# Attention's steps interleaved by hand with its output projection, and layer two's plain products dealt out anew

## Chip, cores and metric

One core of one Trainium2 chip runs the whole program in one launch. The metric is the device time in microseconds (us) of that launch. Engines: TensorE (PE) multiplies matrices, VectorE (DVE), ScalarE (ACT) and GpSimd (POOL) work on elements, SyncE (SP) issues most DMAs. Each engine runs its own instructions strictly in their order and waits at an instruction until what it needs is there.

## What is computed

An inference step of a two-layer encoder, for a prompt of 2048 tokens and, with its own states and caches, a sample of 32 tokens; width 1024. Layer one is a gated delta rule with a short convolution; it isn't touched here. Layer two is attention over a window of chunks of 64 tokens (the own chunk and the two before it), 16 query heads on 4 shared key/value heads of 64 numbers, with a learned sink in each softmax and a gate:

```python
def sink_softmax(s, sinks):
    sk = sinks.astype(jnp.float32)[..., None, None]
    m = jnp.maximum(s.max(-1, keepdims=True), sk)
    p = jnp.exp(s - m)
    return p / (p.sum(-1, keepdims=True) + jnp.exp(sk - m))
...
def swa_layer(x, k, v, pos, cached, w_in, sinks, w_out, ln_g, ln_b):
    b, l, _ = x.shape
    proj = x @ w_in
    q = rope_partial(proj[..., :B_QW].reshape(b, l, B_Q_HEADS, B_HD), pos) * (B_HD ** -0.5)
    q = q.reshape(b, l, B_KV_HEADS, B_GROUP, B_HD)
    z = proj[..., B_QW:]
    sk = sinks.reshape(B_KV_HEADS, B_GROUP)
    o = cached_attention(q, k, v, sk) if cached else banded_attention(q, k, v, sk)
    out = (o * jax.nn.silu(z)) @ w_out
    return layer_norm(DN_ALPHA * x + out, ln_g, ln_b)
```

## The kernel before

**Stages.** Layer one's projections run to about 600 us, the delta rule to about 1190, layer one's output projection, together with layer two's products, to about 1763, attention with layer two's output projection to the end. The program is written piece by piece and a scheduler orders each engine's instructions, except inside a `manual_schedule` of an engine, where the order of the code holds.

**Layer two's products** (class `P2`). The results are ten units: four of the gate z (`z`, 0 to 3), four of the queries (`q`), one of the keys (`k`), one of the values (`v`), each for five blocks of 416 tokens. Block 0 is done *plainly*: a unit is 4 steps of 12 matmuls 128x416 (`product`, L1279 to L1281; each product of two split numbers takes three matmuls: high with high, low with high, high with low). Blocks 1 and 2, and blocks 3 and 4, are done as *pairs* with seven products in place of eight; their operands xs_h, xs_l are first prepared by VectorE and ScalarE (`load_pair`). Weights come through a ring of 12 tiles (`load`, ScalarE's DMA queue). `sequence` lists the units, and the generator `late` hands them out step by step: three plain z units, all of the first pair, z3, k and q0 plainly, the second pair, and at the end q1, q2, q3 and v plainly. The call `both(a, b)` runs a's steps between those of the preparation b. The plain steps at the end are spread over attention's first four chunks.

**Attention** (class `Attention`). Chunks are done in the order 10 to 31, then 0 to 9. `load_kv` brings keys (`kT`) and values (`vd`); `start` brings, for two chunks at a time, queries (`qs`) and gates (`zs`). `chunk(n)` goes through p = 0, 1 (two key/value heads each):

- scores S (L1612): four matmuls in 64-row halves, 128 query rows against 192 keys;
- `softmax`: VectorE's maximum nm (L1487, L1488), ScalarE's four exponentials P (L1495) with their sums, VectorE's es and sm (L1496 to L1499: the sink's share, the sum and its reciprocal);
- GpSimd multiplies P by the reciprocal (L1620, two of 128x384);
- TensorE transposes P (L1627, two groups of three), ScalarE copies one group (L1629), VectorE the other (L1631);
- values ot (L1633): three matmuls of 128 columns against `vd`, in which each chunk's values stand twice, on a diagonal, beside zeros;
- VectorE multiplies by the gate into graw (L1636).

Two chunks make a tile of 128 tokens, put on `pend`. `flush(keep)` then calls `finish` for the oldest tile: ScalarE rounds g_hi (L1508), GpSimd takes g_lo (L1509); for each of two halves of 512 columns TensorE does 8 x 3 matmuls 128x512 into po (L1520 to L1522), VectorE adds the residual (L1523) and takes statistics (L1524); then the normalization (helper lines L466 and L468 for its power, nb L1530, ScalarE's r L1531) and GpSimd's two multiplications with the tables (L1532, L1533) and the store of y. po has one bank of PSUM (pool `u_pp`, one buffer), so a half can't begin before L1523 of the half before has read it. The last tile's end is done by VectorE (L1537, L1539). The sample comes behind chunk 9. The scheduler places all of this, TensorE's order too. The output weights (16 pieces of 128x1024) and the tables load through SyncE's queue when the products' pools are closed (`open_right`).

Of the kernel before, what the change touches and what calls it, by code (L numbers as in the profile page):

```python
# [1133 lines left out]
class P2:  # L1134
# [10 lines left out]
    def __init__(self, tc, right, mid, I, O, T, G):  # L1145
# [108 lines left out]
    def load(self, most=2):  # L1254

        for _ in range(most):
            if self.loads and len(self.held) < self.RING:
                what, slot = self.loads.pop(0)
                w = self.wp.tile([128, 2, 4, 128], F32R, tag="w", name="w")
                src = self.T["w2"][UNITS.index(what[:2]), SLOTS.index(slot)]  # L1260
                self.nc.scalar.dma_start(w[:].rearrange("p s k c -> p s (k c)").bitcast(F32), src)
                self.held.append((what, slot, w))
# [20 lines left out]
    def units(self, units):  # L1283

        self.loads = [(u, s) for u in units for s in self.slots(u)]
        self.held = []
# [139 lines left out]
class Attention:  # L1426


    def __init__(self, tc, left, I, O, T, G):
# [9 lines left out]
        self.turn = 0  # L1439
        self.kT = one.tile([128, 2, NP], F32, tag="kT", name="kT")  # L1440

        self.vd = one.tile([128, 32, 2, 128], F32, tag="vd", name="vd")
        self.nsk = one.tile([128, 8], F32, tag="nsk", name="nsk")
# [7 lines left out]
        self.pend = []  # L1451
        self.data = {}

    def open_right(self, right):
        tc, I = self.tc, self.I
# [5 lines left out]
        rest = load_out_weights(self.nc, self.oone, self.T["wo"][1], self.nc.sync)  # L1461
        self.w = next(rest)
        drain(rest)

    def tables(self):
        self.tabs = ln_tables(self.nc, self.oone, self.I["b_ln_g"], self.I["b_ln_b"])

    def load_kv(self, a, z):
        nc, T = self.nc, self.T
        nc.sync.dma_start(self.kT[:, :, a * 64:z * 64], T["bk"][:, :, a * 64:z * 64].rearrange("a p t -> p a t"))  # L1470
        src = T["bv"][0:NP, :].rearrange("(c k) (p d) -> k c p d", k=64, p=2)
# [6 lines left out]
    def scores_tile(self):  # L1478
        self.turn += 1
        return self.ps_s[self.turn % len(self.ps_s)].tile([128, 2, 2, 256], F32, tag="S", name="S")  # L1480

    def softmax(self, S, P, nskc):
# [3 lines left out]
        nm = thr.tile([128, 4], F32, tag="nm", name="nm")  # L1486
        V.tensor_reduce(out=nm[:, :nsub], in_=S, axis=AX.X, op=ALU.max, negate=True)  # L1487
        V.tensor_tensor(out=nm[:, :nsub], in0=nm[:, :nsub], in1=nskc, op=ALU.min)  # L1488
        sm = thr.tile([128, 4], F32, tag="sm", name="sm")
        es_ = thr.tile([128, 4], F32, tag="es", name="es")  # L1490
        for u in range(nsub):
            src = S[:, u, :]
            if len(P[u].shape) == 3:
                src = src.rearrange("r (j k) -> r j k", k=64)
            nc.scalar.activation(P[u], src, AF.Exp, bias=nm[:, u:u + 1], scale=1.0, accum_out=sm[:, u:u + 1])  # L1495
# [6 lines left out]
    def finish(self, t0, n, graw, late=False, tail=False):  # L1502
        nc, V, pool = self.nc, self.nc.vector, self.otwo
# [5 lines left out]
        nc.gpsimd.tensor_tensor(out=glo[:, :, :n], in0=graw[:, :, :n], in1=ghi[:, :, :n], op=ALU.subtract)  # L1509
        st = pool.tile([128, 2, 6], F32, tag="st", name="st")  # L1510
        w, tabs = self.w, self.tabs
        both = self.scores_tile() if late else None
        for c in range(2):
            cs = slice(c * 512, c * 512 + 512)
            if late:
# [3 lines left out]
            for k in range(KC):  # L1519
                nc.tensor.matmul(ps[:n], ghi[:, k, :n], w[0][k][:, cs], start=(k == 0), stop=False)  # L1520
                nc.tensor.matmul(ps[:n], ghi[:, k, :n], w[1][k][:, cs], start=False, stop=False)  # L1521
                nc.tensor.matmul(ps[:n], glo[:, k, :n], w[0][k][:, cs], start=False, stop=(k == KC - 1))  # L1522
            V.scalar_tensor_tensor(out=r[:n, cs], in0=r[:n, cs], scalar=ALPHA, in1=ps[:n], op0=ALU.mult, op1=ALU.add)  # L1523
            V.bn_stats(out=st[:n, c, :], in_=r[:n, cs])  # L1524
        mv = pool.tile([128, 2], F32, tag="mv", name="mv")
        V.bn_aggr(out=mv[:n], in_=st[:n])
        rs = rsqrt_power(nc, self.G, pool, mv[:n, 1:2], n, 1, "ln", LN_EPS)
        if not tail:
# [4 lines left out]
            nc.gpsimd.tensor_tensor(out=r[:n], in0=r[:n], in1=tabs[1][:n], op=ALU.add)  # L1533
        else:
            for c in range(2):
                cs = slice(c * 512, c * 512 + 512)
                V.scalar_tensor_tensor(out=r[:n, cs], in0=r[:n, cs], scalar=mv[:n, 0:1], in1=tabs[0][:n, cs],  # L1537
                                       op0=ALU.subtract, op1=ALU.mult)
                V.scalar_tensor_tensor(out=r[:n, cs], in0=r[:n, cs], scalar=rs[:n, 0:1], in1=tabs[1][:n, cs],  # L1539
                                       op0=ALU.mult, op1=ALU.add)  # L1540
        nc.sync.dma_start(self.O["y"][t0:t0 + n, :], r[:n])

    def sample(self):
        nc, V, I, T = self.nc, self.nc.vector, self.I, self.T
        one, two, thr, ident = self.one, self.two, self.thr, self.G["ident"]
        ks = one.tile([128, 2, 160], F32, tag="ks", name="ks")
        nc.sync.dma_start(ks[:, :, 0:128], I["cache_kT"].rearrange("a p t -> p a t"))
        nc.sync.dma_start(ks[:, :, 128:160], T["bk"][:, :, NP:NT].rearrange("a p t -> p a t"))
        vc = one.tile([128, 256], F32, tag="vc", name="vc")
        nc.sync.dma_start(vc[:], I["cache_v"])  # L1550
        vn = one.tile([32, 256], F32, tag="vn", name="vn")
        nc.sync.dma_start(vn[:], T["bv"][NP:NT, :])
        qs = two.tile([128, 8, NS], F32, tag="qs", name="qs")
        zs = two.tile([128, 8, 128], F32, tag="zs", name="zs")
        nc.sync.dma_start(qs[:], T["bq"][:, :, NP:NT].rearrange("h p t -> p h t"))
        nc.sync.dma_start(zs[:, :, :NS], T["bz"][:, :, NP:NT].rearrange("h p t -> p h t"))
        graw = thr.tile([128, 8, 128], F32, tag="graw", name="graw", bufs=4)
        for p in range(2):
            ot = self.ps_o.tile([128, 2, 2, 128], F32, tag="ot", name="ot")
            S = self.scores_tile()  # L1560
            for half in range(2):
                hs = slice(half * 64, half * 64 + 64)
                nc.tensor.matmul(S[:, half, 0, :160], qs[hs, p * 4:p * 4 + 4, :], ks[hs, p, :], start=True, stop=True)
            P = thr.tile([128, 2, 384], F32, tag="P", name="P")
            sm = self.softmax(S[:, :, 0, :160], [P[:, 0, :160], P[:, 1, :160]], self.sks[:, p * 2:p * 2 + 2])
            nc.gpsimd.tensor_tensor(out=P[:, :, :160], in0=P[:, :, :160],
                                    in1=sm[:, 0:2].unsqueeze(2).to_broadcast([128, 2, 160]), op=ALU.mult)
            for half in range(2):
                g = p * 2 + half
                hs = slice(half * 64, half * 64 + 64)  # L1570
                gs = slice(g * 64, g * 64 + 64)
                tr = self.ps_t.tile([128, 3, 128], F32, tag="tr", name="tr")
                pt = thr.tile([128, 6, 128], F32, tag="pt", name="pt")
                nc.tensor.transpose(tr[:, 0, :], P[:, half, 0:128], ident[:, :])
                nc.tensor.transpose(tr[:32, 1, :], P[:, half, 128:160], ident[:, :])
                nc.scalar.copy(pt[:, 0, :], tr[:, 0, :])
                V.tensor_copy(pt[:32, 1, :], tr[:32, 1, :])
                oo = ot[hs, 0, 0, :]
                nc.tensor.matmul(oo, vc[:, gs], pt[:, 0, :], start=True, stop=False)
                nc.tensor.matmul(oo, vn[:, gs], pt[:32, 1, :], start=False, stop=True)  # L1580
            of = ot[:, 0, 0, :].rearrange("p (t k) -> p t k", t=4)
            V.tensor_tensor(out=graw[:, p * 4:p * 4 + 4, :NS], in0=of, in1=zs[:, p * 4:p * 4 + 4, :NS], op=ALU.mult)
        self.pend.append((NP, NS, graw))

    def start(self, n):

        nc, T = self.nc, self.T
        if n % 2 == 0:
            qs = self.two.tile([128, 2, 8, 64], F32, tag="qs", name="qs")
            zs = self.two.tile([128, 8, 128], F32, tag="zs", name="zs")  # L1590
            for i in range(2):
                tk = (n + i) * 64
                nc.sync.dma_start(qs[:, i], T["bq"][:, :, tk:tk + 64].rearrange("h p t -> p h t"))
            nc.sync.dma_start(zs[:], T["bz"][:, :, n * 64:n * 64 + 128].rearrange("h p t -> p h t"))
            graw = self.thr.tile([128, 8, 128], F32, tag="graw", name="graw", bufs=4)
            self.data = qs, zs, graw

    def chunk(self, n):
# [38 lines left out]
        if n % 2 == 1:  # L1637
            self.pend.append(((n - 1) * 64, 128, graw))
# [285 lines left out]
```

## Time and profile before

| | us |
|---|---|
| three runs | 2213.85, 2208.47, 2205.18 |
| median | 2208.47 |
| the profiled execution's own time | 2207.43 |
| its span, first to last instruction | 2205.6 |
| TensorE busy in the span | 2101.2 (95%) |
| VectorE, ScalarE, GpSimd busy | 1486.4, 912.1, 713.6 |
| mean granted TensorE clock | 0.987 |

Columns of the profile's lines: in the table by stretch a row has the stretch, its length, then busy time and instruction count of PE, of PE's weight loads, DVE, ACT and POOL, the TensorE clock that was granted (1 is full speed), the DMA engines' share and GB/s. A row of the grouped view has line, engine, operation, output and inputs, shape, count, then busy time, mean ns of one, and the engine's idle time just before it with what ended it. Rows of the timeline and of the chain have start, length and what ran; SPq is SyncE's queue, issuing DMAs. A matmul's listed length contains its passage through the array; the distance between starts is what it costs in a row of them.

### The profile page before, as it was taken

How to read it: one execution, taken by the hardware profiler on the slowest of the kernel's cores; microseconds unless marked ns; L12 is line 12 of the kernel's file. 1: busy time of each engine (PE TensorE's matmuls, PEld its weight loads, DVE VectorE, ACT ScalarE, POOL GpSimd, SP SyncE). 2: the span in 40 equal slices, each digit the busy share in tenths (PEclk: the TensorE clock that was granted, in tenths of full speed). 3: DMA queues.
4: the chain of work that ended last, by engine and by line, in shares of the span. 5: the costliest groups of instructions: out<-in, count | busy, mean ns of one | idle time of the engine just before them, and what ended most of it. 6: DMA issues, size and time to landing. Idle time of an engine off the chain costs nothing.

```text
span 2205.6 us, 37189 instructions
## 1 busy us (share of the span) xinstructions
PE 2101.2 (95%) x13370; PEld 1911.0 (87%) x13370; DVE 1486.4 (67%) x2771; ACT 912.1 (41%) x2405; POOL 713.6 (32%) x1176
## 2 busy tenths in 40 slices
PE   8999999999989999998888999899899988999997
PEld 6999999999979899887776888899899976888775
DVE  5889877776557589888865665555835566556663
ACT  5545545544412477677741111311311135444441
POOL 1212211161111288788841210000000025565663
PEclk9999999999999999999999999999999999999999
DMA  7756656567765635436737765888788895333321
GB/s 282 225 185 195 222 168 196 178 192 239 245 213 158 209 130 172 159 124 208 225 108 262 231 205 167 298 280 283 266 278 279 276 301 137 106 87 96 89 79 43
DMA packets 348377, 430.00 MB, mean 195 GB/s; under 512 B 78352, under 2 KB 276080, under 8 KB 348176
## 3 DMA queue, kind: packets, MB, share of 16 engines
q1 hardware_dynamic: 311280, 310.22, 44.3%
q10 hardware_dynamic: 36912, 117.40, 16.0%
q8 instruction: 106, 1.74, 0.3%
q14 instruction: 79, 0.65, 0.1%
HBM read 269.45 MB, written 158.44 MB: 194 GB/s over the span
## 4 chain that ended last, share of the span: by engine, by line
PE 69%; DVE 12%; POOL 5%; DMA 5%; ACT 4%; issue 3%; SPq 1%; ACTq 0%; DVEq 0%; POOLq 0%
PE ps L77 7%; PE ps L79 7%; PE ps L78 7%; PE ps L1279 5%; PE ps L1280 5%; PE ps L1281 5%; PE ot L1633 3%; PE po L1520 3%; PE po L1521 3%; PE S L1612 3%; PE po L1522 3%; PE po L1052 2%; PE po L1054 2%; PE po L1053 2%; PE tr L1627 2%
## 5 line engine op out<-in xcount | busy, mean ns | idle before, releaser
L77 PE MATMUL ps<-act_hi,w_hi 128*128 128x416 f32 x1280 | 457.2, 357 | 9.5 <-ACT w_hi L53 3.6
L79 PE MATMUL ps<-act_hi,w_lo 128*128 128x416 f32 x1280 | 449.5, 352 | 4.2 <-POOL w_lo L54 3.5
L78 PE MATMUL ps<-act_lo,w_hi 128*128 128x416 f32 x1280 | 450.0, 352 | 0.0
L77 PEld LDWEIGHTS ps<-act_hi,w_hi 128*128 128x128 f32 x1280 | 241.2, 188 | 13.7 <-ACT w_hi L53 4.2
L79 PEld LDWEIGHTS ps<-act_hi,w_lo 128*128 128x128 f32 x1280 | 241.2, 188 | 8.9 <-POOL w_lo L54 4.7
L78 PEld LDWEIGHTS ps<-act_lo,w_hi 128*128 128x128 f32 x1280 | 241.7, 189 | 2.7
L1279 PE MATMUL ps<-xs_h,w 128*128 128x416 f32 x560 | 200.0, 357 | 11.6 <-DVE ra L1336 7.6
L1280 PE MATMUL ps<-xs_l,w 128*128 128x416 f32 x560 | 200.3, 358 | 2.9 <-DVE xs_l L1182 2.9
L1281 PE MATMUL ps<-xs_h,w 128*128 128x416 f32 x560 | 198.9, 355 | 0.0
L54 POOL TENSOR_TENSOR w_lo<-w_raw,w_hi 128x1024 fp32r<-128x1024 f32 x32 | 81.0, 2530 | 357.6 <-ACT w_hi L53 343.6
L295 DVE SCALAR_TENSOR_TENSOR y<-R,convw,y 128x2083 f32<-128x2083 f32 (+2 forms) x78 | 175.3, 2247 | 24.4 <-ACT y L293 24.2
L585 POOL TENSOR_TENSOR tm<-L,Tt 128x60 f32<-128x60 f32 (+19 forms) x375 | 136.3, 363 | 87.2 <-PE sp L760 50.0
L588 POOL TENSOR_TENSOR Tt<-Tt,tm 128x60 f32<-128x60 f32 (+19 forms) x375 | 143.8, 383 | 28.3
L1620 POOL TENSOR_TENSOR P<-P,sm 128x384 f32<-128x384 f32 (+2 forms) x128 | 100.9, 810 | 120.4 <-DVE sm L1499 56.9
L1474 POOL MEMSET vd<- 64x768 f32 (+2 forms) x10 | 7.8, 779 | 398.2 <-DVE ra L1336 397.9
L1495 ACT ACTIVATE P<-S,nm 128x192 f32<-128x192 f32 (+2 forms) x260 | 104.8, 420 | 61.6 <-DVE nm L1488 49.0
L1279 PEld LDWEIGHTS ps<-xs_h,w 128*128 128x128 f32 x560 | 106.8, 191 | 14.6 <-DVE ra L1336 8.3
L1336 DVE SCALAR_TENSOR_TENSOR ra<-ps,u 128x416 f32<-128x416 f32 x60 | 35.4, 590 | 123.3 <-PE ps L1281 121.9
L1052 PE MATMUL po<-wo,g_hi 128*128 128x512 f32 (+1 forms) x272 | 111.0, 408 | 6.9 <-DVE r L1057 6.0
L1280 PEld LDWEIGHTS ps<-xs_l,w 128*128 128x128 f32 x560 | 106.5, 190 | 5.6 <-DVE xs_l L1182 4.2
L1281 PEld LDWEIGHTS ps<-xs_h,w 128*128 128x128 f32 x560 | 107.2, 191 | 1.3
L1054 PE MATMUL po<-wo,g_lo 128*128 128x512 f32 (+1 forms) x272 | 107.4, 395 | 0.0
(298 smaller groups left out, 4755.5 us busy)
## 6 DMA issues: line engine op xcount, KB each, us to landing
w<-s_w ACTq DMA_DIRECT2D x180, 512.0 KB, 4.7
s_w<-pre_hl SPq DMA_DIRECT2D x160, 256.0 KB, 2.5
w_raw<-in_w_in SPq DMA_DIRECT2D x32, 512.0 KB, 6.5
s_wo<-pre_hl SPq DMA_DIRECT2D x64, 256.0 KB, 4.0
gb<-s_gcum SPq DMA_DIRECT2D x34, 256.0 KB, 5.1
k<-s_k SPq DMA_DIRECT2D x34, 256.0 KB, 3.7
s_z<-z SPq DMA_DIRECT2D x40, 208.0 KB, 2.0
s_q<-y SPq DMA_DIRECT2D x8, 1024.0 KB, 5.2
```

The source lines that it names most:

```text
L77: nc.tensor.matmul(ps, hi[:, k, :], xh[:, k, :], start=(k == 0), stop=False)
L78: nc.tensor.matmul(ps, hi[:, k, :], xl[:, k, :], start=False, stop=False)
L79: nc.tensor.matmul(ps, lo[:, k, :], xh[:, k, :], start=False, stop=(k == KC - 1))
L295: self.nc.vector.scalar_tensor_tensor(out=y[:, a:z], in0=R[:, a + j:z + j], scalar=self.convw[:, i, j:j + 1], in1=y[:, a:z], op0=ALU.mult, ...
L585: P.tensor_tensor(out=tm[:n, i0 - k:, :w], in0=L[:n, i0:, j:j + 1].to_broadcast(sh), in1=Tt[:n, j:j + 1, :w].to_broadcast(sh), op=ALU.mult)
L588: P.tensor_tensor(out=Tt[:n, i0:, :w], in0=Tt[:n, i0:, :w], in1=tm[:n, i0 - k:, :w], op=ALU.subtract)
L1052: nc.tensor.matmul(ps[:n], ghi[:, k, :n], w[0][k][:, cs], start=(k == 0), stop=False)
L1054: nc.tensor.matmul(ps[:n], glo[:, k, :n], w[0][k][:, cs], start=False, stop=(k == KC - 1))
L1279: nc.tensor.matmul(ps, w[:, 0, k], xh[:], start=first and k == 0, stop=False, skip_group_check=True)
L1280: nc.tensor.matmul(ps, w[:, 0, k], xl[:], start=False, stop=False, skip_group_check=True)
L1281: nc.tensor.matmul(ps, w[:, 1, k], xh[:], start=False, stop=last and k == 3, skip_group_check=True)
L1495: nc.scalar.activation(P[u], src, AF.Exp, bias=nm[:, u:u + 1], scale=1.0, accum_out=sm[:, u:u + 1])
```

## The change

It does three things.

1. *Plain units.* All four z units come ahead of the first pair, ten of their steps beside its preparation (six before); v, k and q0 come ahead of the second pair; q1, q2 and q3 remain for attention.
2. *Output weights.* The ring of weight tiles lives to the end; behind the last unit's weights it takes 12 of the 16 pieces of output weights, so that `open_right` loads 4 pieces and the tables.
3. *Attention.* `chunk` is taken apart into `scores`, `turn` (transposes and copies) and `values`, and TensorE's order is written out by hand for the whole stage. Chunks 10, 11 and 12 run beside the remaining plain steps (`alone`). From chunk 13 on, `beside(n)` gives TensorE the scores of chunk n for both p, six po matmuls, `turn(n-1, 0)`, six po, `turn(n-1, 1)`, six po, `values(n-1)`, six po. The other engines' order is still the scheduler's. Values take two matmuls per pair of chunks (`vp`, 128 keys, no zeros, a new load of 2 MB in all) and two for the single chunk (`vd`), each of 64 columns, the two in different halves of the columns. GpSimd's multiplies become one of 128x4x128 and one of 128x2x2x64 for each p. The sample stands between chunk 31 and chunk 0. g_hi and g_lo are made half a tile ahead (`ready`). The last tile's y is stored in halves through two queues.

The diff, cut (`start`, `softmax` and the sample's branches keep what they computed):

```diff
@@ P2
+        self.wp = new_pool(tc, ring, "p2_w", self.RING, side="right")
-        self.wp = new_pool(tc, right, "p2_w", self.RING, side="right")
...
+                if what is None:
+                    flat = w[:].rearrange("p s k c -> p (s k c)")
+                    self.nc.scalar.dma_start(flat.bitcast(F32), self.T["wo"][1][slot // 2, :, slot % 2])
+                    self.out.append(flat)
...
-        self.loads = [(u, s) for u in units for s in self.slots(u)]
+        self.loads = [(u, s) for u in units for s in self.slots(u)] + [(None, i) for i in range(self.RING)]
@@ Attention
+        both = T["bv"][a * 64:z * 64, :].rearrange("(c k) d -> k c d", k=128)
+        nc.sync.dma_start(self.vp[:, a // 2:z // 2, :], both)
...
+                if pair is not None:
+                    part = flat[:, :, at:at + 128]
+                    nc.gpsimd.tensor_tensor(out=part, in0=part, in1=sm[:].unsqueeze(2).to_broadcast([128, 4, 128]),
+                                            op=ALU.mult)
...
+    def values(self, n):
...
+                if pair is not None:
+                    for h in range(2):
+                        hs = slice(h * 64, h * 64 + 64)
+                        nc.tensor.matmul(ot[hs, p], self.vp[:, pair, p * 128 + h * 64:p * 128 + h * 64 + 64],
+                                         pt[:, 2 * h:2 * h + 2, :], start=True, stop=one is None)
+                if one is not None:
+                    for h in range(2):
+                        hs = slice(h * 64, h * 64 + 64)
+                        nc.tensor.matmul(ot[hs, p], self.vd[:, one, p, hs], pt[:, 4:6, :],
+                                         start=pair is None, stop=True)
...
+    def alone(self, n):
+
+        self.scores(n, (0,))
+        for f in self.left_over[:1]:
+            f()
+        yield
+        for f in self.left_over[1:]:
+            f()
+        yield
+        self.scores(n, (1,))
+        self.turn(n, 0)
+        yield
+        self.left_over = [lambda: self.turn(n, 1), lambda: self.values(n)]
+        yield
+
+    def beside(self, n):
+
+        self.scores(n)
+        next(self.out)
+        for f in self.left_over:
+            f()
+            next(self.out)
+        self.left_over = [lambda: self.turn(n, 0), lambda: self.turn(n, 1), lambda: self.values(n)]
...
+            for j in self.finish(*got, last):
+                if j >= 4 and ahead is None and self.pend:
+                    ahead = self.ready()
+                yield
...
+                if k % 2 == 1 and k < KC - 1:
+                    yield 4 * c + k // 2
             V.scalar_tensor_tensor(out=r[:n, cs], in0=r[:n, cs], scalar=ALPHA, in1=ps[:n], op0=ALU.mult, op1=ALU.add)
             V.bn_stats(out=st[:n, c, :], in_=r[:n, cs])
+            if c == 0:
+                yield 3
@@ the stage
-    sequence = [("z", j, 0) for j in range(3)] + [p + (1,) for p in pairs]
-    sequence += [("z", 3, 0), ("k", 0, 0), ("q", 0, 0)] + [p + (2,) for p in pairs]
-    sequence += [("q", j, 0) for j in range(1, 4)] + [("v", 0, 0)]
+    sequence = [("z", j, 0) for j in range(4)] + [p + (1,) for p in pairs]
+    sequence += [("v", 0, 0), ("k", 0, 0), ("q", 0, 0)] + [p + (2,) for p in pairs]
+    sequence += [("q", j, 0) for j in range(1, 4)]
...
-        both(itertools.islice(late, 6), p2.load_pair(1))
+        both(itertools.islice(late, 10), p2.load_pair(1))
...
-    order = list(range(10, 32)) + list(range(10))
...
+    order = list(range(10, 32)) + ["s"] + list(range(10))
+    with tc.manual_schedule(engines={ET.PE}):
+        drain(itertools.islice(late, 2))
+        for i in range(3):
+            for _ in att.alone(order.pop(0)):
+                drain(itertools.islice(late, 1))
+            att.load_kv(*((14, 18), (18, 24), (24, 32))[i])
+        drain(late)
+        p2.rest()
+        right.close()
+        att.open_right(right, p2.out)
+        att.load_kv(0, 8)
+        for n in order:
+            att.beside(n)
+        att.rest()
```

More of the change, by code (lines that the diff above doesn't have):

```diff
@@ L1504, in finish, with rest, ready @@
+    def rest(self):
+        for f in self.left_over:
+            f()
+            next(self.out)
+        self.late = True
+        drain(self.out)
+    def ready(self):
+        nc, pool = self.nc, self.otwo
+        t0, n, graw = self.pend.pop(0)
         r = pool.tile([128, D], F32, tag="r", name="r")
@@ L1509, in finish, with outs @@
         nc.gpsimd.tensor_tensor(out=glo[:, :, :n], in0=graw[:, :, :n], in1=ghi[:, :, :n], op=ALU.subtract)
+        return t0, n, r, ghi, glo
+    def outs(self):
+        while not self.pend:
+            yield
+        got = self.ready()
+        while got is not None:
+            ahead = None
+            last = self.late and not self.pend
+            for j in self.finish(*got, last):
+                if j >= 4 and ahead is None and self.pend:
+                    ahead = self.ready()
+                yield
+            while ahead is None and not self.late:
+                if self.pend:
+                    ahead = self.ready()
+                else:
+                    yield
+            if ahead is None and self.pend:
+                ahead = self.ready()
+            got = ahead
+    def finish(self, t0, n, r, ghi, glo, tail):
+        nc, V, pool = self.nc, self.nc.vector, self.otwo
         st = pool.tile([128, 2, 6], F32, tag="st", name="st")
         w, tabs = self.w, self.tabs
-        both = self.scores_tile() if late else None
+        both = self.scores_tile() if self.late else None
         for c in range(2):
             cs = slice(c * 512, c * 512 + 512)
-            if late:
+            if both is not None:
                 ps = both[:, c].rearrange("p u k -> p (u k)")
@@ L1539, in finish @@
                 V.scalar_tensor_tensor(out=r[:n, cs], in0=r[:n, cs], scalar=rs[:n, 0:1], in1=tabs[1][:n, cs],
                                        op0=ALU.mult, op1=ALU.add)
[L1541 to L1596, printed above, removed]
@@ L1640, in flush @@
-    def flush(self, keep):
-        while len(self.pend) > keep:
-            self.finish(*self.pend.pop(0), late=(keep == 0), tail=(keep == 0 and len(self.pend) == 0))
+                queue.dma_start(self.O["y"][t0:t0 + n, cs], r[:n, cs])
+        yield 7
 class Filler:
@@ L1758, in program @@
     att.load_kv(8, 14)
[L1759 to L1782 removed]
+    order = list(range(10, 32)) + ["s"] + list(range(10))
[13 more added lines that the diff above has]
+        att.rest()
     left.close()
     right.close()
+    ring.close()
 def make_consts(tc, I, pool):
```

245 lines of the change are left out of this document (154 added, 91 removed).

## The prediction

> **What bounds the kernel now.** First the table by stretch of time (stretch, its length, busy time of each engine with its instruction count, granted TensorE clock, DMA share, GB/s), for the stages that the change touches: layer two's products up to about 1763, attention and its out-projection behind them.
>
> ```profile
> 1600.00:1750.00 150.00, 149.73 (x785) 147.18 (x785) 70.82 (x141) 20.78 (x42) 0.00 (x0) 0.99 0.85 278
> 1900.00:2100.00 200.00, 200.00 (x1097) 159.16 (x1096) 123.37 (x294) 94.52 (x365) 122.08 (x113) 1.00 0.34 94
> 2150.00:2206.00 56.00, 44.03 (x199) 30.14 (x197) 16.57 (x34) 6.58 (x10) 21.56 (x17) 0.95 0.12 43
> ```
>
> TensorE is the bound: in steady attention it never rests, while VectorE works 62% and GpSimd 61% of the time. A product's matmul costs 150/785 = 0.19 us, a plain step of 12 of them 2.29. So time can be won in TensorE's holes, in its work, or in the tail. The holes, by the same view on narrower stretches:
>
> ```profile
> 1384.00:1394.00 10.00, 3.25 (x12) 2.09 (x11) 9.39 (x19) 5.96 (x14) 0.00 (x0) 0.73 0.88 296
> 1388.00:1399.00 11.00, 6.25 (x16) 5.03 (x17) 9.68 (x20) 6.18 (x13) 0.00 (x0) 0.53 0.84 286
> 1798.00:1833.00 35.00, 23.93 (x150) 17.01 (x148) 20.72 (x50) 17.13 (x80) 10.49 (x14) 0.99 1.03 346
> 1833.00:1839.00 6.00, 5.95 (x25) 4.20 (x26) 5.16 (x11) 4.97 (x18) 5.60 (x5) 0.50 1.23 258
> ```
>
> The first pair starts with 6.75 us of rest, and attention's start, while output weights still load, has 35 - 23.93 = 11.1. Behind each the clock stands at half for some 5.5 us (0.53, 0.50), which costs about 2.75 more. Now the steady pattern, from the chain of waits (start, length, what):
>
> ```profile
> 1961.33 0.85 PE S L1612 x8
> 1968.96 1.29 PE ot L1633 x6
> 1970.25 0.66 PE tr L1627 x6
> 1971.15 0.23 PE po L1520
> 1972.52 1.18 PE S L1612 x12
> 1983.32 1.50 PE S L1612 x16
> 1994.44 1.50 PE S L1612 x16
> ```
>
> A chunk takes 11.0 us (1972.52 to 1994.44 are two): scores 1.50, twelve transposes 1.32, twelve passes of values 2.58, 24 out-projection matmuls at 0.229 = 5.5. That is 10.9: the stage is TensorE's own work.
>
> **Part by part: holes.** *Plain products.* z3's four steps (9.2 us) now run while the first pair's operands are prepared, where TensorE rested 6.75 us and then lost half of 6.25 busy us to the slow clock, 9.9 together. I take -8.5 (between -4 and -9.9). The second pair now has v ahead of it, whose steps need no gate multiply on VectorE: -1.
>
> *The first scores.* On TensorE at the end of the second pair, before (xs: products of the pair; x_h, x_l: plain products; S: scores of chunk 10):
>
> ```order
> 7515 L1281 MATMUL ps<-xs_h,w 128x416
> 7516 L1281 MATMUL ps<-x_h,w 128x416
> 7517 L1279 MATMUL ps<-x_h,w 128x416
> 7518 L1280 MATMUL ps<-x_l,w 128x416
> ...
> 7613 L1279 MATMUL ps<-x_h,w 128x416
> 7614 L1612 MATMUL S<-kT,qs 128x192 x4
> ```
>
> and after:
>
> ```order
> 7529 L1286 MATMUL ps<-x_h,w 128x416
> 7530 L1284 MATMUL ps<-xs_h,w 128x416
> ...
> 7552 L1285 MATMUL ps<-xs_l,w 128x416
> 7553 L1286 MATMUL ps<-xs_h,w 128x416
> 7554 L1565 MATMUL S<-kT,qs 128x192 x4
> 7555 L1284 MATMUL ps<-x_h,w 128x416
> ```
>
> The 98 plain matmuls that stood between the last pair product and the scores now stand behind the scores. What the scores wait for, by the timeline of TensorE and of SyncE's queue:
>
> ```profile
> 1762.88 0.35 PE L1281 MATMUL ps<-xs_h,w 128*128 128x416 f32 x1
> 1781.56 0.76 PE L1612 MATMUL S<-kT,qs 64*128 64x192 f32 x6
> 1768.85 0.34 SPq L1418 DMA_DIRECT2D s_bq<-ra  x1
> 1769.24 0.91 SPq L1448 DMA_DIRECT2D sks<-in_sinks_s  x2
> 1770.25 0.39 SPq L1470 DMA_DIRECT2D kT<-s_bk  x1
> 1770.73 2.64 SPq L1476 DMA_DIRECT2D vd<-s_bv  x4
> 1774.08 1.42 SPq L1593 DMA_DIRECT2D qs<-s_bq  x2
> ```
>
> The store of the last rotated unit goes 5.8 us behind the last pair product, and sinks (three instead of two), keys, the new pair values, values and queries queue behind it: 5.8 + 0.3 + 1.4 + 0.5 + 0.5 + 2.7 + 1.4 = 12.6, and the queries must land: 2.1 to 4 us. Before, this ran under the 18.7 us of plain steps; now TensorE waits. I take 15 us, and 2.75 for the clock: +17.7 (ends +11 and +20). The steps aren't lost, they cover chunks 10 to 12.
>
> *The first out-projection.* Chunk 13's scores are followed by the first six po matmuls, which need g_hi and g_lo, and these are queued behind chunk 13's exponentials on ScalarE and its four probability multiplies on GpSimd. The grouped view:
>
> ```profile
> L1495 ACT ACTIVATE P<-S,nm 128x192 f32<-128x192 f32 x240 | 98.0, 425 | 56.1 <-DVE nm L1488 46.0 <-PE S L1612 4.7 <-PE po L1522 3.7
> L1620 POOL TENSOR_TENSOR P<-P,sm 128x384 f32<-128x384 f32 x120 | 97.0, 831 | 116.8 <-DVE sm L1499 55.8 <-DVE es L1496 44.0 <-ACT a L1318 16.6
> L1495 ACT ACTIVATION_READ_ACCUMULATOR P<-S,nm 128x1 f32 x260 | 54.4, 209 | 0.0
> L1487 DVE TENSOR_REDUCE nm<-S 128x4 f32<-128x768 f32 x60 | 57.0, 951 | 12.6 <-PE S L1612 12.2
> L1509 POOL TENSOR_TENSOR g_lo<-graw,g_hi 128x1024 fp32r<-128x1024 f32 x16 | 38.1, 2384 | 3.9 <-ACT g_hi L1508 3.8
> L1532 POOL TENSOR_TENSOR r<-r,ln_g 128x1024 f32<-128x1024 f32 x15 | 36.0, 2398 | 6.2 <-ACT r L1531 6.2
> L1523 DVE SCALAR_TENSOR_TENSOR r<-r,po 128x512 f32<-128x512 f32 x30 | 20.6, 687 | 27.2 <-PE po L1522 26.9
> ```
>
> From the scores' start: maximum at 2.1, eight exponentials at 0.634 and their small operations to 7.7, second multiplies (1.7) to 9.9, g_lo 2.4 to 12.3, against a wish at 1.5: 10.8 us and 2.75 of slow clock, 13.5. It takes the place of the old 11.1 + 3: -0.6.
>
> **Part by part: work and tail.** *Values.* The zero-padded 128-column matmuls (12 passes of 0.215) become 16 passes of 64 columns in two column halves. If the halves run side by side they take 8 x 0.215 = 1.72, and about 0.4 for entering and leaving the other tile shape: 2.12 against 2.58, -0.46 a chunk, -15 for 32. This kernel's one 64-column group:
>
> ```profile
> L696 PE MATMUL bps<-ta,npr x256: 218/218/267, 768.1 to 1139.1; 64*64 64x64 f32 x128
> ```
>
> I take the overlap as holding for 128 rows as for 64; without it the values cost 3.44 + 0.4, +1.26 a chunk. The Trainium skill ("TensorE: Matmul & The Clock Gate", Part 3) gives 2.38-fold for three column tiles; an estimate by that efficiency is 2.2 + 0.4 us, so the gain would vanish (+15 on my sum). Each chunk's scores now stand in one burst; where they stood apart the chain shows 0.85 for half a chunk, so -0.2 a chunk: -6 (0 to -12).
>
> *The tail.* The end of the chain before:
>
> ```profile
> 2188.78 0.48 PE S L1522 x2
> 2192.78 1.25 ACT r L1531
> 2194.10 2.40 POOL r L1532
> 2196.57 2.33 POOL r L1533
> 2199.57 0.98 POOLq L1895
> ```
>
> The sample rows' normalization (1.25 + 2.40 + 2.33 + 0.98) stands ahead of the last tile's; with the sample in the middle it goes: -7 (-4 to -9).
>
> **The part that decides: the one po bank.** The out-projection has one accumulator bank. Every chunk now ends a half tile right behind its scores, has six transposes, and starts the next half, which must wait for VectorE to empty the bank. VectorE's rows after, the same in every chunk (nm: maximum; es: sink term; L1734 empties po):
>
> ```order
> 1954 L1498 TENSOR_REDUCE nm<-S 128x4
> 1955 L1499 TENSOR_TENSOR nm<-nm,nsk 128x4
> 1956 L1504 TENSOR_TENSOR es<-nm,nsk 128x4
> 1957 L1498 TENSOR_REDUCE nm<-S 128x4
> 1958 L1499 TENSOR_TENSOR nm<-nm,nsk 128x4
> 1959 L1504 TENSOR_TENSOR es<-nm,nsk 128x4
> 1960 L1734 SCALAR_TENSOR_TENSOR r<-r,po 128x512
> ```
>
> The emptying stands behind both halves' maxima. With T the scores' start: first reduction at T+0.97, nm, es, the second with its own, emptying from 3.45 to 4.14; TensorE is ready at 1.50 + 1.37 + 0.66 = T+3.55. So at least 0.65 us are lost a chunk. And it can be more, by VectorE's and GpSimd's timelines of one chunk before:
>
> ```profile
> 1984.69 0.94 DVE L1487 TENSOR_REDUCE nm<-S 128x4 f32<-128x768 f32 x1
> 1985.67 0.16 DVE L1488 TENSOR_TENSOR nm<-nm,nsk 128x4 f32<-128x4 f32 x1
> 1986.62 1.54 DVE L1496 TENSOR_TENSOR es<-nm,nsk 128x4 f32<-128x4 f32 x1
> 1985.75 2.39 POOL L1533 TENSOR_TENSOR r<-r,ln_b 128x1024 f32<-128x1024 f32 x1
> ```
>
> es works on 128x4 numbers as nm does (0.16), and takes 1.54: it ends at 1988.16, where GpSimd's operation ends (1988.14). The Trainium skill ("SBUF — State Buffer", "Who interferes with whom") has the rule: a VectorE instruction with two SBUF inputs and a GpSimd one that reads SBUF exclude each other for the whole instruction; the row agrees. In the new order nm and es stand ahead of the emptying, so their waits are TensorE's. GpSimd after (P: probability multiplies):
>
> ```order
> 984 L1584 TENSOR_TENSOR P<-P,sm 128x4x128
> 985 L1588 TENSOR_TENSOR P_18903<-P,sm 128x2x2x64
> 986 L468 TENSOR_TENSOR ln_y<-ln_y,half 128x1
> 987 L1745 TENSOR_TENSOR r<-r,ln_g 128x1024
> 988 L1746 TENSOR_TENSOR r<-r,ln_b 128x1024
> 989 L1584 TENSOR_TENSOR P<-P,sm 128x4x128
> ...
> 993 L1693 TENSOR_TENSOR g_lo<-graw,g_hi 128x1024
> ```
>
> The two table operations (987, 988) follow a normalization that ends with the values of the odd chunk, so by my walk they run from T+0.4 to T+5.2 of the even one: nm waits to 2.9, es to 5.3, the emptying ends at 7.3, 3.8 us late. In odd chunks g_lo ends at about T+2.4: 1.0 late. If the table operations come a microsecond earlier or later the even stall is 2.4 or 4.8; none if they miss. I take 3.0 and 1.0, 2.0 a chunk, times 28 chunks: **+56** (18 without any such wait, 67 by the full walk).
>
> **Sum.** 2207.4 of the profiled execution - 9.5 (products) + 17.7 - 0.6 (holes) - 21 (work) - 7 (tail) + 56 = 2243; the median of the runs is 1 us over the profiled time, so 2244.
>
> **Rivals.** *Quick emptying (not slower).* Place: L1734 of each chunk. If VectorE gets the first reduction sooner, or the maxima overlap more than I count, it ends by T+3.6 and the stall falls to 0 to 10 us in all: 2207.4 - 20.4 + 0 to 10 = 2187 to 2197. It decides from 0.4 us a chunk downwards. For it, by the waits of TensorE before:
>
> ```profile
> PE po L1520 <- DVE r L1523: 0.5, 1, 0.5
> ```
>
> There the same bank cost 0.5 us in all, over 30 halves. Against: the halves' ends weren't tied to the scores then, nor the emptying to a place behind the maxima. *No port waits.* The table operations fall behind L1734 (start after T+3.3): the stall is 18, the time 2206, no change. For it: in before nm's mean over 64 is 328 ns (row below), near the unblocked 160, so most escaped. Against: GpSimd's new order puts them ahead of the even chunk's multiplies every time.
>
> ```profile
> L1488 DVE TENSOR_TENSOR nm<-nm,nsk 128x4 f32<-128x4 f32 x64 | 21.0, 328 | 0.9
> ```
>
> *Full walk.* Every even chunk 3.8: the stall is 67, the time 2255. *Halves one after the other.* +1.72 a chunk on any of these: 2244 + 55 = 2299. *The re-dealing does nothing* (the pair's start waits for something else): +8 on each.
>
> **Numbers.** My forecast with the full walk 0.50, no port waits 0.23, quick emptying 0.22, column halves 0.05. About 0.5%, 11 us, is what a measurement of this kernel can tell from no change. Faster by more takes the quick case and little of the next: 0.24; within: 0.20; slower: 0.56. The range is 2190 to 2262: it leaves out the lower half of the quick case and the serial halves. The forecast's own is 2225 to 2262.
>
> **What would show it.** Waits of TensorE: po L1729 on DVE r L1734 some 50 us in all (under 15 refutes the decisive step); the mean of nm and es several times 160 ns; a hole of 12 to 17 us between the last xs product and the first scores, one of about 10 ahead of the first po, on g_lo; no hole at the first pair; values at 0.11 a pass (0.215 refutes the overlap); 9 us behind the last matmul.

## The result and the profile after

The changed kernel takes 2302.22 us (median of four runs, 2297.77 to 2310.16) beside 2211.16 before in the same comparison: a ratio of 1.0423, 95% interval 1.0399 to 1.0447. It is slower by 91 us, far outside the range of 2190 to 2262. Its profiled execution took 2297.77, with a span of 2296.0 and a mean clock of 0.973.

First the table by stretch of the kernel after, for the first pair's start, the start of attention and its steady part:

```profile
1384.00:1399.00 15.00, 14.51 (x76) 13.74 (x74) 13.79 (x28) 8.75 (x19) 0.00 (x0) 1.00 0.84 287
1399.00:1450.00 51.00, 46.34 (x240) 44.81 (x241) 17.40 (x34) 11.13 (x25) 0.00 (x0) 0.97 0.90 310
1800.00:1850.00 50.00, 30.20 (x174) 23.82 (x175) 20.63 (x60) 16.02 (x64) 13.65 (x15) 0.81 0.98 270
1900.00:2100.00 200.00, 169.65 (x998) 121.32 (x997) 108.89 (x253) 82.52 (x314) 104.10 (x98) 0.97 0.26 73
2100.00:2250.00 150.00, 121.05 (x678) 82.19 (x677) 83.58 (x183) 57.01 (x224) 71.99 (x64) 0.92 0.24 67
```

The hole at the first pair is gone (14.51 of 15 busy), though 4.7 us of rest come up behind it (0.45 in the same stretch before), 3.7 of them a wait for VectorE's addition of pair products (`ra`, L1341). In steady attention TensorE, busy throughout before, now rests 15% and then 19% of the time, at a clock that is no longer 1.00. What it waits for there, and at attention's start, by the waits of TensorE (engine and line waited for, us in all, times, longest):

```profile
PE po L1729 <- DVE r L1734: 38.5, 20, 4.5
PE ot L1639 <- DVE graw L1648: 19.2, 31, 0.6
PE S L1565 <- DMA qs<-s_bq: 15.5, 1, 15.5
PE tr L1615 <- POOL P L1584: 9.0, 2, 8.2
PE po L1729 <- DVE sm L1506: 7.8, 9, 0.9
PE po L1729 <- ACT g_hi L1692: 7.0, 1, 7.0
PE S L1565 <- ACT P L1503: 5.8, 2, 3.4
PE po L1729 <- DVE sm L1507: 1.8, 1, 1.8
PE po L1731 <- POOL g_lo L1693: 1.2, 1, 1.2
PE S L1729 <- DVE r L1734: 0.8, 1, 0.8
PE ot L1644 <- DVE graw L1648: 0.6, 1, 0.6
PE ot L1630 <- DVE graw L1648: 0.5, 1, 0.5
```

The waits of po, put down to L1734 and to the sm operations that follow it, are 48.9 us in all: the decisive step of the prediction, which had 56. The 20.3 us of ot for the gate multiply stood nowhere in it. One chunk, from the chain of waits:

```profile
2014.10 0.58 PE ot L1639 x4
2014.68 0.46 PE ot L1644 x4
2015.16 0.44 DVE graw L1648
2015.73 0.65 PE ot L1639 x4
2018.41 0.87 PE S L1565 x8
2020.30 1.69 DVE nm L1499
2023.38 0.70 DVE r L1734
2024.12 0.68 PE po L1729
2024.81 0.43 PE po L1730
2025.23 0.43 PE po L1731
```

Eight passes of values take 0.58 + 0.46 = 1.04 us, 0.13 a pass with the change of tile shape: the two column halves do run side by side, and the rival of serial halves is refuted, though its 2299 lies next to the measured time. Then TensorE stands 0.6 us until VectorE has read the first pair's half of the bank. Behind the scores nm takes 1.69, and after that stall (2.0 us) po matmuls start 0.43 apart, not 0.23: the granted clock is 0.50 from 2024.27 to 2027.69. Why nm takes so long, from VectorE's and GpSimd's timelines of the same chunk:

```profile
2020.30 1.68 DVE L1499 TENSOR_TENSOR nm<-nm,nsk 128x4 f32<-128x4 f32 x1
2019.57 2.39 POOL L1746 TENSOR_TENSOR r<-r,ln_b 128x1024 f32<-128x1024 f32 x1
```

nm ends at 2021.98, where GpSimd's table operation ends (2021.96).

### The profile page after: what moved, and what is told of

Same layout as the page of the kernel before. It is cut to its first block, busy times and chain, and to the rows that moved or that the text cites. A ratio compares the mean times of both kernels' runs of the same rounds, so it can differ in the third digit from the quotient of the medians.

```text
span 2296.0 us, 37342 instructions
## 1 busy us (share of the span) xinstructions
PE 2105.5 (92%) x13494; PEld 1885.2 (82%) x13494; DVE 1492.8 (65%) x2769; ACT 913.2 (40%) x2405; POOL 712.7 (31%) x1172
## 4 chain that ended last, share of the span: by engine, by line
PE 66%; DVE 16%; DMA 5%; POOL 4%; ACT 3%; issue 3%; SPq 2%; ACTq 0%; DVEq 0%; POOLq 0%
PE ps L77 8%; PE ps L79 8%; PE ps L78 8%; PE ps L1284 5%; PE ps L1285 5%; PE ps L1286 5%; PE po L1729 3%; PE po L1052 2%; PE po L1054 2%; PE po L1053 2%; PE po L1731 2%; PE po L1730 2%; DVE nm L1498 2%; POOL Tt L588 2%; PE ot L1639 2%
## 5 line engine op out<-in xcount | busy, mean ns | idle before, releaser
L1729 PE MATMUL po<-w,g_hi 128*128 128x512 f32 (+1 forms) x192 | 91.0, 474 | 55.2 <-DVE r L1734 38.5
L1584 POOL TENSOR_TENSOR P<-P,sm 128x512 f32<-128x512 f32 x62 | 64.6, 1041 | 193.9 <-DVE sm L1507 127.8
L1052 PE MATMUL po<-wo,g_hi 128*128 128x512 f32 (+1 forms) x272 | 111.9, 412 | 5.7 <-DVE r L1057 4.7
L1341 DVE SCALAR_TENSOR_TENSOR ra<-ps,u 128x416 f32<-128x416 f32 x60 | 35.4, 590 | 125.4 <-PE ps L1286 118.5
L1284 PEld LDWEIGHTS ps<-xs_h,w 128*128 128x128 f32 x560 | 106.2, 190 | 10.0 <-DVE ra L1341 7.7
L1053 PE MATMUL po<-wo,g_hi 128*128 128x512 f32 (+1 forms) x272 | 108.0, 397 | 0.0
```

What stands on the lines that cost most here:

```text
L1284: nc.tensor.matmul(ps, w[:, 0, k], xh[:], start=first and k == 0, stop=False, skip_group_check=True)
```

## Experiments

Theory A: the written order makes TensorE wait for VectorE twice in every chunk (for the emptying of po behind the maxima, and for the gate multiply between the two pairs' values); GpSimd's operations lengthen the first wait, and the slow clock follows it. Rival B: these waits are slack in front of a softmax chain that would end late anyway. Times are medians beside 2302; ratios are to the kernel before, timed beside each run.

**Gate multiplies last.** In `values`:

```diff
+        gates = []
...
-            V.tensor_tensor(out=graw[:, p * 4:p * 4 + 4, sl], in0=of, in1=zs[:, p * 4:p * 4 + 4, sl], op=ALU.mult)
+            gates.append((of, sl))
+        for p, (of, sl) in enumerate(gates):
+            V.tensor_tensor(out=graw[:, p * 4:p * 4 + 4, sl], in0=of, in1=zs[:, p * 4:p * 4 + 4, sl], op=ALU.mult)
```

> Theory A (the hand-written order makes TensorE wait for VectorE twice a chunk): the second key/value pair's values wait for the gate multiply that reads the first pair's from the same bank, 20 us in all; with both multiplies behind all eight matmuls these waits fall under 2 us and the time falls by 15 to 25, to 2277 to 2287 us. Rival B (the waits are slack: what counts is the softmax chain that ends later anyway): the 20 us turn up as more waiting for the emptying of po, and the time stays within 6 us of 2302.

Measured: 2289.29, ratio 1.0357 [1.0335, 1.0380]. The waits of ot for L1648 are gone from the list, but those of po grew from 48.9 to 58.8 (L1734 is L1737 in this kernel):

```profile
PE po L1732 <- DVE r L1737: 44.8, 20, 4.8
PE po L1732 <- DVE sm L1506: 11.0, 9, 1.2
PE po L1732 <- DVE sm L1507: 2.2, 1, 2.2
PE S L1732 <- DVE r L1737: 0.8, 1, 0.8
```

So 20 us of waiting were removed and ten came back at the other place. The gain is 13, between what A and B expected. The rests ahead of the emptying grew from 2.0 to between 2.6 and 2.9 us in the eight even chunks from 16 to 30, every one of them is followed by half clock, and the granted clock between 1900 and 2100 fell from 0.97 to 0.94: slow clock took a part of the gain as well.

**Halves end ahead of the scores.** The first tile starts a chunk later, which shifts every end of a half tile from behind the scores to ahead of them:

```diff
-        next(self.out)
+        if n != 13:
+            next(self.out)
         for f in self.left_over:
             f()
-            next(self.out)
+            if n != 13:
+                next(self.out)
```

> The first tile starts one chunk later (three steps later), so that every half tile ends ahead of a chunk's scores and not behind them; the same work otherwise. Theory A: waits for the emptying of po fall from 49 us to under 8, the clock stays at 1.00 in the steady stage, and the first out-projection no longer waits for g_hi and g_lo (8 us): 2302 - 41 - 24 (slow clock) - 8 to 10 = 2220 to 2235 us. Rival B: the maxima wait behind the emptying instead, probabilities come late, transposes wait for GpSimd; less than 30 us are gained, 2270 or more.

Measured: 2262.81, ratio 1.0229 [1.0202, 1.0256]: 39 gained, between A (67 or more) and B (under 30). The waits for the emptying fell to 2.4 and the steady clock is 1.00, as A has it, but others took their place:

```profile
PE ot L1639 <- DVE graw L1648: 25.5, 30, 1.7
PE tr L1615 <- ACT pt L1617: 11.6, 20, 0.8
PE S L1731 <- DVE r L1736: 2.4, 2, 1.6
1900.00:2100.00 200.00, 178.57 (x1095) 125.20 (x1092) 115.47 (x275) 84.05 (x328) 114.36 (x104) 1.00 0.32 85
```

The gate multiplies' waits have grown by some 6 us, and transposes now wait for ScalarE to copy the bank before them; its copy stands behind four exponentials.

**Without the table operations** (left out: both multiplications with the normalization's tables on GpSimd, for all tiles but the last).

```diff
-            nc.gpsimd.tensor_tensor(out=r[:n], in0=r[:n], in1=tabs[0][:n], op=ALU.mult)
-            nc.gpsimd.tensor_tensor(out=r[:n], in0=r[:n], in1=tabs[1][:n], op=ALU.add)
```

> Leaves out the two multiplications with the normalization's tables on GpSimd for all tiles but the last. Theory A with the port waits: nm's mean falls from 529 to under 250 ns, the waits for the emptying of po from 49 us to 20 to 28 (the 0.65 us of each chunk and g_lo's share), stalls of over 3 us and the slow clock behind them go: 2302 - 21 to 29 - 15 to 22 = 2250 to 2266 us. Rival (the order of VectorE's rows alone makes the stalls, GpSimd has no part): 2290 or more, nm unchanged.

Measured: 2261.07, in a single run: 41 gained, as Theory A has it. nm went from this row of the changed kernel

```profile
L1499 DVE TENSOR_TENSOR nm<-nm,nsk 128x4 f32<-128x4 f32 x64 | 33.8, 529 | 1.9
```

to the first of these, and the waits of po for L1734 from 38.5 to the second:

```profile
L1499 DVE TENSOR_TENSOR nm<-nm,nsk 128x4 f32<-128x4 f32 x64 | 16.3, 254 | 1.9
PE po L1729 <- DVE r L1734: 11.2, 19, 1.0
1900.00:2100.00 200.00, 179.40 (x1096) 127.70 (x1095) 105.02 (x273) 87.71 (x329) 74.07 (x87) 1.00 0.30 84
```

With the sm rows (7.8 and 1.8, unchanged) the waits of po are 20.8. GpSimd's table operations thus made 28 of the 49 us, and all of the slow clock in the steady part (1.00 from 1900 to 2250 without them, 0.97 and 0.92 with them): the order of VectorE's rows alone costs 0.7 a chunk, near the 0.65 of the prediction.

**Both edits on order together.**

> The first two edits together. Theory A: the two waits are independent, the gains add: 2200 to 2215 us, TensorE busy over 98% in the steady stage. Rival B: no better than the second edit alone.

Measured: 2240.53, ratio 1.0130 [1.0105, 1.0155]. The edits' own gains are 13 and 39, together they give 62, more than the sum, yet less than the 87 or more that Theory A expected; TensorE is not over 98% busy, since the wait for ScalarE's copies, 11.6 with the second edit alone, has grown to

```profile
PE tr L1615 <- ACT pt L1617: 22.2, 24, 2.0
```

**Transposes first.** The first transposes of the chunk before go ahead of the scores, and two po steps in a row behind the second ones:

```diff
+        first, then = self.left_over[:-2], self.left_over[-2:]
+        for f in first:
+            f()
         self.scores(n)
-        if n != 13:
-            next(self.out)
-        for f in self.left_over:
+        steps = (0, 0, 0) if n == 13 else (1, 2, 1)
+        drain(itertools.islice(self.out, steps[0]))
+        for f, some in zip(then, steps[1:]):
             f()
-            if n != 13:
-                next(self.out)
+            drain(itertools.islice(self.out, some))
```

> The kernel with gate multiplies last and half tiles ending ahead of the scores, and on TensorE the first transposes of the chunk before put ahead of the scores, with two po steps in a row between the second transposes and the values. The new wait of that kernel is 22 us of transposes waiting for ScalarE's copy out of the bank, which stands behind four exponentials. Theory: with the transposes a step earlier ScalarE copies before the exponentials; these 22 us fall under 5: 2240 - 15 to 20 = 2220 to 2225. Rival: the second copy, or the values, then wait for ScalarE in the same way, less than 6 us gained.

Measured: 2216.57, ratio 1.0029 [1.0017, 1.0041]. 24 gained, a little more than expected. The 22 us are gone; 8.3 remain, of values for the second copy.

**The new deal alone** (the kernel before with the changed `sequence`, ten steps beside the first pair and three per chunk at attention's start).

> The kernel before with the plain products dealt out as in the change and nothing else (ten steps beside the first pair's preparation; the twelve that remain go three, not four, to each of attention's first four chunks). The term of the prediction: 6.75 us of rest and the slow clock behind it go at the first pair, about 1 us at the second: -9.5, 2199 to 2202 us beside 2210. Rival: the 9 us of steps that covered the start of attention are missed there, where TensorE waits for the first queries and for output weights; what is gained is given back, 2207 to 2212.

Measured: 2223.86, ratio 1.0057 [1.0039, 1.0075]: slower. The rival holds, and more. In the profiled execution TensorE rests 14.8 us between 1750 and 1850 (11.1 before), and from 1900 to 2100, where it never rested, it now rests 2.7 and does 1072 matmuls in place of 1097. So the start is not all of the loss: the order that the scheduler finds for attention's steady part is slower too, and no run separates the two.

**The old deal under the new attention** (z3 ahead of the second pair, v last, six steps ahead of the first scores).

> The changed kernel with the plain products dealt out as before (z3 ahead of the second pair, v at the end, six steps beside the first pair's preparation; six in place of two of the then 16 remaining ahead of the first scores). Theory: the products lose the 6 us that the new deal won, and the three steps that now stand between the last pair product and the first scores cover 7 of the 15.5 us of that wait: 2302 + 6 - 7 = 2297 to 2304, so the deal is worth nothing in the end and the loss is all attention's. Rival: the deal itself made a good part of the loss by baring the start of attention; 2285 or less.

Measured: 2311.87, ratio 1.0472 [1.0437, 1.0507]. Neither expectation fits: the old deal is worse here. A wait of 11.1 us of scores for ScalarE's copy of v's transposes (L1408) stands in its list, which was not foreseen. So the deal costs about 13 us outside the change and nothing inside it (there it may be worth some 10, but the interval touches that of the changed kernel); the loss is attention's.

**Output weights through SyncE's queue.**

```diff
-                    self.nc.scalar.dma_start(flat.bitcast(F32), self.T["wo"][1][slot // 2, :, slot % 2])
+                    self.nc.sync.dma_start(flat.bitcast(F32), self.T["wo"][1][slot // 2, :, slot % 2])
```

> The changed kernel with the 12 early pieces of output weights issued from SyncE's queue and not from ScalarE's. Theory: chunk 10's and 11's exponentials and sink terms stand behind those issues in ScalarE's queue, and one issue waits 7 us for another transfer; the 8.2 us wait of the transposes for GpSimd's P goes, with about 2.5 us of slow clock: 2302 - 9 to 12 = 2290 to 2293. Rival: the issues wait for their ring place in SyncE's queue as long, keys and values behind them come later, and the time stays at 2298 to 2306.

Measured: 2301.33, ratio 1.0416 [1.0400, 1.0432]: nothing gained. The time is the rival's, but not for its reason, since the scores' wait is unchanged (15.3). The transposes' 8.2 us are gone, but the first out-projection waits for g_hi longer by more than that (7.0 before):

```profile
PE po L1729 <- ACT g_hi L1692: 17.6, 1, 17.6
```

By the profile what holds g_hi itself back there is the store of rotated queries (`s_bq<-a`), which now stands in SyncE's queue with the output weights: ScalarE is idle for 11.8 us ahead of g_hi until that transfer ends. In the changed kernel it waits for the same store, for 2.5 us:

```profile
1837.70 7.29 DMA s_bq<-a
1845.02 1.05 ACT g_hi L1692
```

**The start changed**, on the kernel with transposes first: output weights through SyncE, chunk 10's queries ahead of its values (`att.start(10)` before `load_kv`), and `islice(late, 6)` for 2 ahead of the first scores.

> The same with the start of attention changed: output weights through SyncE's queue, chunk 10's queries loaded ahead of its values, and six plain steps in place of two ahead of the first scores. Theory: of the 16 us that the first scores wait, 9.2 are covered and 4 are gone from the queue, and the 8 us behind ScalarE's queue go with the slow clocks: 18 to 24 us under the kernel with the transposes first, 2198 to 2207. Rival: the four steps are missed between chunks 10 to 12, where TensorE then waits for the softmax of each; less than 8 us gained.

Measured: 2203.04, ratio 0.9973 [0.9958, 0.9989]: 13.5 gained, of 18 to 24 expected; the scores still wait 8.4 us for keys.

**Values last.** On the same, `(1, 3, 0)` for `(1, 2, 1)`.

> The kernel with the start changed, and the values of the chunk before put behind the last po step of a chunk and not ahead of it. There the values wait 8.3 us in all for ScalarE's second copy, which stands behind exponentials. Theory: 1.4 us more between transposes and values let the copy end: these waits fall under 2 and the time by 5 to 8: 2195 to 2198 beside 2203. Rival: the gate multiplies then end later and meet the emptying of po on VectorE; nothing gained (2200 to 2206).

Measured: 2195.08, ratio 0.9943 [0.9923, 0.9963]: 8 gained, as expected, and faster than both kernels, though by half a percent only. The waits for the second copy did not fall under 2 but to 4.7. Its steady stage:

```profile
1900.00:2100.00 200.00, 197.63 (x1251) 143.65 (x1251) 156.71 (x324) 101.63 (x393) 129.02 (x119) 1.00 0.35 95
1960.74 1.50 PE S L1565 x16
1971.31 0.88 PE S L1565 x8
1982.48 0.53 PE S L1565 x4
```

Chunks of 10.57 and 11.17, 10.87 in the mean. The kernel before took 11.51 in each of the nine chunks between the first scores of these rows of its chain, and 11.0 in the two that the prediction read.

```profile
1849.20 0.85 PE S L1612 x8
1952.82 0.85 PE S L1612 x8
```

**First loads from ScalarE's queue**, on that.

> The kernel with values last, and the first queries, gates, keys and values of attention issued from ScalarE's queue, so that they don't stand behind the last store of rotated queries in SyncE's. Theory: the first scores' wait (8.4 us for keys) goes almost wholly, with 2.5 us of slow clock: 8 to 11 under the kernel with values last, 2185 to 2190. Rival: the loads wait as long for memory that the pair's tiles still hold, and ScalarE's work behind them comes later: no gain.

Measured: 2196.54, ratio 0.9945 [0.9920, 0.9970]: no gain. The scores wait for the sinks, which were still in SyncE's queue, in place of the keys (9.5 us before, as the first row; after, the other two):

```profile
PE S L1565 <- DMA kT<-s_bk: 9.5, 1, 9.5
```

```profile
PE S L1565 <- DMA sks<-in_sinks_s: 6.7, 1, 6.7
PE S L1565 <- DMA qs<-s_bq: 2.6, 1, 2.6
```

## Why the prediction was right in its direction and wrong in its size

The step named as decisive held in its place: 48.9 us of waits for the emptying of po against 56, made as it said by the order of VectorE's rows (0.7 a chunk without GpSimd's tables; the prediction's own times give 4.14 - 3.55 = 0.59 for its 0.65) and by GpSimd's operations (28 us, shown by leaving them out). That the size came so near is in part luck: 3.0 was taken for every second chunk, while these rests were mostly 2.0 up to chunk 31, and 4.0 to 4.5 in chunks 3, 5, 7 and 9 behind the sample (in chunk 3 g_lo and both table operations run on GpSimd without a pause, from 2148.16 to 2155.27).

What failed is the sum around it. It had no term for TensorE's waits at other places (the gate multiply above all), priced the slow clock behind the two big holes only, and took too much for the tail and the products. To see what each is worth, take TensorE from the last pair product to the last matmul, before and after:

```profile
1762.88:2196.15 433.27, 419.58 (x2268) 331.24 (x2266) 253.50 (x603) 183.67 (x699) 232.00 (x219) 0.99 0.42 119
1764.52:2287.98 523.46, 415.56 (x2350) 298.15 (x2348) 259.44 (x602) 182.91 (x693) 232.69 (x216) 0.92 0.36 100
```

It rests 13.7 and 107.9 us. Matmuls ran at half clock for 6.2 and 49.6 us (the trace's clock records laid over its matmuls), of which half is lost: 3.1 and 24.8. What is left is work: 416.5 and 390.8. For the profiled execution 2243 was predicted and 2297.8 measured; the 55 us, term by term:

- *Holes behind the products*: 15 taken for the first scores, 15.5 measured, +0.5. The first po: 10.8 taken, 7.0 + 1.2 measured, -2.6. Its mechanism was right in part: chunk 13's exponentials end at 1842.5, and from there ScalarE waits for the store named above.
- *po bank*: -7.1.
- *Not in the sum, the gate multiply*: +20.3. The working followed each tile from chunk to chunk, but not the one bank that both pairs' values share. Before, the same bank was read between the pairs too, with other TensorE work there; the change put the pairs back to back. That TensorE waits here for the multiply was shown by moving both multiplies behind the values. No run gave each pair a bank of its own.
- *Not in the sum, transposes that wait for P at the start*: +9.0. The chain shows ScalarE's queue in it:

```profile
1794.79 9.09 DMA vd<-s_bv
1803.95 0.33 ACTq L1262
1804.32 0.21 ACT es L1505
```

By the profile an issue of output weights waits on that queue for a transfer of values to end, and the sink term of chunk 10's softmax stands behind it. The prediction went through SyncE's queue and not through ScalarE's, to which the change had added twelve issues. Taking the issues off that queue removed the wait, but by itself no time, since g_hi's then grew.
- *Rests of before that stayed*: +3.2. The old hole of 11.1 was taken as replaced; but 5.8 us of scores waiting for exponentials remain at the start after, while 2.6 us of other rests went.
- *Mis-sized, the clock*: +19.2. The loss grew by 21.7, and 2.5 net was taken. 17.7 us of it lie behind 1850, in eight stretches of half clock, for which the sum had nothing; without GpSimd's table operations none of the eight is left. The Trainium skill ("TensorE: Matmul & The Clock Gate", table at the end) advises against rests of more than about 3 us. Here the four rests of 4.0 to 4.5 us in this part were all followed by half clock, and so were four of the eight rests of 2.0 to 2.3 us between 1850 and 2100, as in the chunk above.
- *Work*: +1.8. -21 taken; 25.7 less was measured, of which 6.5 are the 34 plain matmuls done earlier, so -19.2. This term held; values took 1.04 + 1.08 = 2.12 a chunk, as predicted, though the 0.4 in it for the change of tile shape stood without a row. But the prediction's 11.0 a chunk is read from two chunks that were shorter than the row of chunks before them (11.51).
- *Products*: +4.6. -9.5 taken; the last pair product starts at 1764.52 (1762.88 before), with 34 more plain matmuls done ahead of it: 6.5 - 1.6 = 4.9 gained. At the first pair the 3.7 us wait for `ra` came in place of the hole; at the second pair, where 1 us was taken, that wait fell from 7.2 to 3.3.
- *Tail*: +5.5. -7 taken; behind the last matmul 9.5 us passed before and 8.0 after, so 1.5 gained. The sample rows' normalization had run mostly beside the last tile's matmuls, which end at 2196.15; behind it stood only the last tile's power operation, which started at 2198.88 in place of 2197.84. The prediction's own sign, 9 us behind the last matmul, already held before.

These add up to 54.4. The decisive term, the gate multiply and the clock behind 1850 are shown by runs; the other terms are worked out from rows of the two profiles. The remaining 3 us between 2302 - 2244 and these 55 are the distance of the profiled execution from the median.

Of the rivals, quick emptying and no port waits are refuted by the rows of po and nm; serial halves by the passes of values. A second bank for po, which might take away the decisive wait, was not tried.

## What to carry to other kernels

When an engine's order is written by hand, walk every accumulator bank through it, not only the one that is scarce: each place where the engine comes back to a bank needs other work ahead of it, long enough for the slowest reader, with what that reader may wait for itself. Remove one such wait and look at the list again, for here each of four edits uncovered or left a next wait in the same list, and only all of them together made the new order faster than the old. A short idle time of TensorE costs more than its length once the clock falls behind it.

## What the runs showed of the hardware

- Two column halves of 128 rows and 64 columns run side by side: 16 passes of 256 in 2.12 us, 0.13 each, against 0.215 for a full-width pass.
- A VectorE operation on 128x4 numbers, both inputs in SBUF, took 1.68 us in the chunk above and 2.28 in another (at 2150.59) while a GpSimd table operation ran, and 0.16 right behind it; without GpSimd's table operations nm's mean halved, 529 to 254 ns.
- In attention's steady part four of eight rests of 2.0 to 2.3 us were followed by a stretch of 3.4 us at half clock, and all four of 4.0 to 4.5 us by one of 6.8.
